# Sample-token projections with the tokens as stationary operand, in four PSUM quadrants, of a two-layer hybrid decoder step

## The chip, the cores and the metric

One Trainium2 chip; the program runs on one of its cores. The metric is the device time of one execution in microseconds, the median of several runs.

## The reference

One inference step of a two-layer decoder on two groups that share the weights: a prompt (2048 tokens) and sample tokens (8 sequences of 4, so 32 tokens). Layer 0 is gated linear attention with 4 heads, layer 1 sliding-window grouped-query attention with 4 groups; between them shared keys and values are projected once.

```python
u = rmsnorm(h, norm_g)                 # (tokens, 1024), prompt and sample alike
proj = u @ w_in                        # layer 0: q 512, k 512, v 2048, gate 2048, g_low 16
log_a = log_sigmoid(g_low @ w_gate2 + b_gate) / 16
o, state = gla_recurrence(q / sqrt(128), k, v, log_a, state0)
h = h + (rmsnorm(o) * silu(gate)) @ w_out          # w_out (2048, 1024)
k, v = rope(rmsnorm(rmsnorm(h) @ w_k)), rmsnorm(h) @ w_v      # 4 KV heads of 64
q, gate = split(rmsnorm(h) @ b_w_in)   # layer 1: 2048 + 2048
h = h + (attend(q, k, v, sinks) * silu(gate)) @ b_w_out
```

The change concerns `u @ w_in`, `u @ w_k`, `u @ w_v`, `u @ b_w_in` and the two products with `w_out` for the 32 sample tokens.

## The kernel before

All float32 products are made of fp16 pairs: a value is a high part plus a low part, and `PASSES` (L283) gives the three products high x high, high x low, low x high. A matmul takes a stationary operand of up to 128 x 128 (loaded by LDWEIGHTS) and streams a moving operand of up to 512 columns past it into one PSUM bank. PSUM banks go by tags: `pj`, `o` and `tr` have two each, `lev` and `kv` one.

**Stage A** (layer 0): the prompt is cut into 4 blocks of 512 tokens, and the outer loop runs over 4 heads x 4 blocks (`blocks`). Per block `qk_steps` projects q and k, `vg_steps` v and gate, `level_steps` and `decay_steps` prepare the recurrence and `chunk_steps` runs it. After the last block of a head the sample tokens of that head are projected (`SampleA.proj_steps`), while the next head's weights arrive: `Unit.load` fetches float32 halves into the ring `wraw` (three buffers), and ScalarE (L197) and VectorE (L198) split them into `W` tiles. A tile scheduler orders each engine's instructions here. `logs` computes the decay, `glow` the low-rank gate, `u_steps` the norm. Then the first output projection runs over 16 chunks (`a_out`), with the sample's part (`out_sample`) at chunk 7 and its end at chunk 10.

**Stage B** (layer 1): 4 groups x 16 chunks, three chunks in flight. The order of TensorE's instructions is pinned to the program's order (`pin`): `ORDER` deals projections ("f") between scores ("A") and values ("B"). After a chunk's round one step of `boundary` runs, among them a whole group's sample projections (`SampleB.proj_steps`), which use the same `W` tiles as the prompt. The second output projection (`Pair.steps`) has the sample's part as `s_out`.

**The sample's projections** are `sproj_steps` (L631). The weights are stationary, 128 input rows by 128 output columns, and the tokens move. Per output tile of 128 columns and k-tile of 128 rows there are two matmuls: the high weights with the tokens' high and low parts side by side (64 columns), and the low weights with the tokens' high part (32 columns). Eight tiles share a bank; the result stands with output columns on the partitions, and `total` (L650) adds the two halves on ScalarE (L656) and VectorE (L657). For the heads and groups the loop runs over 8 k-tiles, for the output projections over 16 or 24; `out_sample` (L1086) then turns its result back to tokens on partitions by four transposes per half.

```python
for k in range(nk):
    wide = lambda: mm(out, w(k, 0), a_[:, kts[k]], start=k == 0, stop=k == nk - 1)
    ...
    mm(out[:, 0, :], w(k, 1), a_[:, kts[k], 0, :], start=False, stop=False)
```

Counted over the program: 10 tiles x 8 k-tiles x 2 per A head, 8 x 8 x 2 per B group (12 x 8 x 2 in the first, which has the shared K/V), and the output projections. Other lines that the steps below touch: L101 is the helper `mm`, L104 the helper `tp` (a transpose by identity), L1039 the one fp32 matmul of the program (`psk`), L1175 a 512-column copy out of PSUM in `q_norm`, L1183 the sum on POOL that makes `kT` there, and `att` the sample attention's scores, which write 32 PSUM partitions per sequence.

Of the kernel before, what the change touches and what calls it, by code (L numbers as in the profile page):

```python
# [19 lines left out]
P = 128  # L20
# [54 lines left out]
def _body(tc, nc, cp, sb, ps, dr, i, o):  # L75
# [24 lines left out]
    def mm(*a, **k):  # L100
        return order(nc.tensor.matmul(*a, **k))  # L101
# [159 lines left out]
    class Cols:  # L261
# [18 lines left out]
        def cols(self, n):  # L280
            return [lambda kt, hl, x=x: self(kt, hl, slice(x * P, (x + 1) * P)) for x in range(n)]

# [347 lines left out]

    def sproj_steps(tiles, nk, act_hi_lo, kts=None, bank=("pj", 2)):  # L631

        box = []
        kts = kts or list(range(nk))

        def one(x, w):
            if x % 8 == 0:
                n = min(8, len(tiles) - x)
                box.append(PT(bank[0], [P, 512], bufs=bank[1])[:, : n * 2 * SMP].rearrange("p (x z t) -> p x z t", z=2, t=SMP))
            out = box[x // 8][:, x % 8]  # L640
            a_ = act_hi_lo()
            for k in range(nk):
                wide = lambda: mm(out, w(k, 0), a_[:, kts[k]], start=k == 0, stop=k == nk - 1)
                if k == 0:
                    wide()
                mm(out[:, 0, :], w(k, 1), a_[:, kts[k], 0, :], start=False, stop=False)
                if k > 0:
                    wide()

        def total(dst, x0, x1, scale):  # L650
            for a in range(x0, x1, 1):
                if a == x0 or a % 8 == 0:
                    b = min(x1, a // 8 * 8 + 8)
                    src = box[a // 8][:, a % 8 : b - a // 8 * 8]
                    d = dst[:, a - x0 : b - x0]
                    act(d, src[:, :, 1], AF.Copy, scale=scale)  # L656
                    dve.scalar_tensor_tensor(d, src[:, :, 0], scale, d, ALU.mult, ALU.add)  # L657

        return [lambda x=x, w=w: one(x, w) for x, w in enumerate(tiles)], total

# [8 lines left out]
    class SampleA:  # L669
# [3 lines left out]
        def proj_steps(self):  # L673
            w = self.w
            st, total = sproj_steps([w.q, w.k] + w.v.cols(4) + w.g.cols(4), KT, lambda: uTs)

            def fin():
                self.qkv = T("sqk", [P, 6, SMP], F32, 1)
                total(self.qkv, 0, 6, DESC * SQ)
                self.sg = T("ssg", [P, 4, SMP], F32, 1)  # L680
                total(self.sg, 6, 10, 1.0)
                silu2(self.sg)

            if self.h == 0:
                st.append(lambda: glow(uTs, SMP, gls))
            return st + [fin]

# [254 lines left out]
    for n, (h, j) in enumerate(blocks):  # L942
# [47 lines left out]
        if n == 0:  # L990
# [22 lines left out]
            dve.tensor_copy(lvs, f_)  # L1013
            id3 = C("id3", [96, SMP], F32)
            later(id3, i["c_id3"])
            bm = C("bm", [96, NS], F32)
# [68 lines left out]

    def out_sample(tiles, half, finish_s, kts=None, sc=OSC):  # L1086
        st, total = sproj_steps(tiles, len(kts or range(16)), lambda: ogTs[0], kts, (("lev", "kv")[half], 1))
# [34 lines left out]
    for c in range(lead, tail):  # L1122
        aout[c + 1][0]()
        weave(aout[c][1][0] + aout[c][1][1], some(each))
        if c == 7:
            late_s = [out_sample(w.cols(4), half, a_finish_s) for half, w in enumerate((wo, wo1))]
# [199 lines left out]
    class SampleB:  # L1326
# [3 lines left out]
        def proj_steps(self):  # L1330
            w = self.w
            first = [x for v in w.kv for x in v.cols(NKV)]
            st, total = sproj_steps(w.q.cols(4) + w.g.cols(4) + first, KT, lambda: uTs)

            def fin():
                if first:
                    t = T("sq1", [P, NKV, SMP], F32, 1)
                    total(t, 8, 12, 1.0)
                    nc.sync.dma_start(skvd, t)
                self.qk = T("sqk", [P, 5, SMP], F32, 1)  # L1340
                nc.sync.dma_start(self.qk[:, 0, :], skvd[:, self.g])
                total(self.qk[:, 1:], 0, 4, 1.0)
                self.sg = T("ssg", [P, 4, SMP], F32, 1)
                total(self.sg, 4, 8, 1.0)
                silu2(self.sg)

            return st + [fin]

# [322 lines left out]

    blks = []
    parts = {}
    boundary = []
# [4 lines left out]
    def s_out(half):  # L1679

        cols = [slice(z * P, (z + 1) * P) for z in range(4)]
        right = [k + 2 for k in UP]
        fs, kts = ((0, 2, 5), UP + UP + right) if half else ((0, 3), UP + right)
        return out_sample([lambda k, hl, z=z: wf[fs[k // 8]](k % 8, hl, z) for z in cols], half, b_finish_s, kts, OSCB)
# [78 lines left out]
def consts():  # L1763
# [22 lines left out]
    for tq in range(2):  # L1786
# [9 lines left out]
        "c_lvs": lvs,  # L1796
        "c_id3": np.tile(np.eye(SMP, dtype=np.float32), (3, 1)),
        "c_bm": np.tile((np.arange(SMP)[:, None] // TS == np.arange(NS)[None, :]).astype(np.float32), (3, 1)),
# [45 lines left out]
```

## Time and profile before

| | |
|---|---|
| three runs | 2857.28, 2862.69, 2869.30 us; median 2862.69 |
| profiled execution | 2863.85 us |
| its span, first to last instruction | 2862.1 us |
| mean granted TensorE clock | 0.983 of full speed |
| TensorE (PE) busy | 96% |
| VectorE (DVE), ScalarE (ACT), GpSimd (POOL) busy | 64%, 50%, 37% |
| DMA | 137 GB/s on the mean |

A row of the timeline gives the start of a group of like instructions and the time to the end of the last; since matmuls are pipelined, what a matmul costs in a row of them is the distance of the starts, not its duration. PE stands for matmuls, PEld for the weight loads beside them.

### The profile page before, as it was taken

The page shows a single profiled execution, that of the slowest core. Times are in us where ns is not written, and L with a number is a line of the kernel's source. Part 1 is how long each engine was busy: PE and PEld are TensorE (multiplying, and loading weights), DVE is VectorE, ACT ScalarE, POOL GpSimd, SP SyncE. Part 2 cuts the span into 40 slices and gives each one's busy share as a digit, 9 for nine tenths or more (in the row PEclk, how much of TensorE's full clock was granted, in tenths as well). Part 3 has the DMA queues.
Part 4 walks back from the last instruction along what each step waited for, and adds up shares of the span by engine and source line. Part 5 has one row for each costly group of instructions (what it writes and reads, how often), then busy time and mean ns, then how long its engine had stood idle before and what let it go on. Part 6 is the DMA issues. An engine that isn't in the chain of part 4 may idle for free.

```text
span 2862.1 us, 51609 instructions
## 1 busy us (share of the span) xinstructions
PE 2735.9 (96%) x19070; PEld 1392.4 (49%) x19070; DVE 1845.7 (64%) x3815; ACT 1440.3 (50%) x3385; POOL 1063.6 (37%) x1471
## 2 busy tenths in 40 slices
PE   6899999999999999999899999999999999988999
PEld 3445444444454444444344555555555555543444
DVE  5767787677768775336413666677777766767653
ACT  6655665466546654333313555566666666641110
POOL 1242233222322321116405676666566556530000
PEclk9899999999999999999999999999999999999999
DMA  8351334124312533799975555866877788798651
GB/s 209 90 124 36 100 101 150 38 82 136 115 38 85 171 84 96 180 240 282 233 193 135 108 130 120 203 117 129 173 116 130 157 155 165 151 236 172 125 112 57
DMA packets 774230, 391.78 MB, mean 137 GB/s; under 512 B 629200, under 2 KB 698776, under 8 KB 773944
## 3 DMA queue, kind: packets, MB, share of 16 engines
q1 hardware_dynamic: 761016, 352.75, 54.6%
q0 software_dynamic: 10880, 35.66, 3.4%
q8 instruction: 149, 2.44, 0.4%
q14 instruction: 105, 0.86, 0.1%
q10 hardware_dynamic: 2080, 0.07, 0.0%
HBM read 138.90 MB, written 107.54 MB: 86 GB/s over the span
## 4 chain that ended last, share of the span: by engine, by line
PE 56%; DVE 12%; DMA 11%; ACT 10%; issue 6%; POOL 4%; SPq 1%; DVEq 0%; ACTq 0%; POOLq 0%
PE pj L101 33%; PE o L101 11%; PE tr L101 8%; PE kv L101 3%; ACT o L1279 2%; DMA pst<-v 2%; DVE v L198 2%; ACT v L197 2%; DMA pre<-pst 1%; PE lev L101 1%; DMA wraw<-in_a_w_in_dram 1%; DVE o L1274 1%; DVE W L198 1%; POOL ogT L195 1%; DVE lev L1274 1%
## 5 line engine op out<-in xcount | busy, mean ns | idle before, releaser
L101 PE MATMUL pj<-W,uT 128*128 128x512 f16 x5088 | 1208.1, 383 | 6.6 <-ACT qT L430 2.9
L101 PEld LDWEIGHTS <-uT 128*128 128x128 f16 x6976 | 654.7, 99 | 714.1 <-issue 40.4
L101 PE MATMUL tr<-W,uT 128*128 128x512 f16 x1536 | 365.8, 379 | 0.0
L186 POOL TENSOR_SCALAR rs_m<-ss 128x1 f32<-128x1 f32 (+3 forms) x190 | 46.1, 243 | 685.7 <-ACT og L611 234.0
L101 PEld LDWEIGHTS <-X 128*128 128x128 f16 x2744 | 185.8, 98 | 149.3 <-issue 14.7
L1279 ACT ACTIVATE o<-o,mx 128x256 f32<-128x256 f32 (+1 forms) x384 | 168.5, 439 | 168.1 <-DVE mx L1274 163.6
L1274 DVE CUSTOM_DVE_ANT_0 o<-o,madd,nsink 128x256 f32<-128x256 f32 (+1 forms) x384 | 184.0, 479 | 48.3 <-PE o L101 44.0
L101 PE MATMUL pj<-uT,W 128*128 128x512 f16 (+1 forms) x912 | 186.0, 354 | 27.0 <-DMA uT<-ogT 24.3
L198 DVE SCALAR_TENSOR_TENSOR v<-o,v 128x512 f16<-128x512 f32 (+1 forms) x192 | 128.8, 671 | 102.0 <-ACT v L197 82.0
L187 POOL TENSOR_TENSOR rs_r<-rs_m,mhalf 128x1 f32<-128x1 f32 (+2 forms) x186 | 184.8, 994 | 14.4
L101 PEld LDWEIGHTS <-W 128*128 128x128 f16 x2448 | 128.0, 98 | 113.1 <-issue 18.5
L101 PEld LDWEIGHTS <-v 128*128 128x128 f16 x976 | 95.2, 98 | 116.0 <-DMA v<-ogd 1.9
L508 POOL TENSOR_TENSOR E<-bt 128x256 f32<-128x256 f32 x96 | 73.9, 770 | 198.4 <-DVE X L195 124.8
L195 POOL TENSOR_TENSOR ogT<-og,ogT 128x512 f16<-128x512 f32 x68 | 88.0, 1295 | 154.4 <-ACT ogT L194 142.5
L101 PEld LDWEIGHTS <-sth 128*128 128x128 f16 x2080 | 111.4, 99 | 52.3 <-DMA sth<-v 12.2
L101 PEld LDWEIGHTS <-sg 128*128 128x128 f16 x800 | 78.6, 99 | 107.5 <-DMA sg<-ogd 12.3
L101 PE MATMUL o<-gl,X 128*128 128x256 f16 (+1 forms) x768 | 114.9, 273 | 5.5 <-DMA X<-qe 5.5
L197 ACT ACTIVATE v<-o 128x512 f16<-128x512 f32 (+1 forms) x192 | 111.3, 579 | 11.1 <-DMA sth<-v 7.6
L101 PE MATMUL kv<-rmask,sth 128*128 128x64 f16 x1984 | 107.0, 194 | 10.1 <-DMA sth<-v 9.2
L101 PE MATMUL kv<-rmask,pst 128*128 128x64 f16 x992 | 102.4, 194 | 9.3 <-DMA pst<-v 9.3
L1279 ACT ACTIVATE lev<-lev,mx 128x256 f32<-128x256 f32 (+1 forms) x128 | 56.5, 441 | 103.3 <-DVE mx L1274 101.2
L101 PE MATMUL pj<-W,v 128*128 128x512 f16 x448 | 104.2, 379 | 1.1 <-DMA v<-ogd 1.1
(468 smaller groups left out, 5092.5 us busy)
## 6 DMA issues: line engine op xcount, KB each, us to landing
pre<-pst POOLq DMA_DIRECT2D x72, 256.0 KB, 3.4
W<-pre SPq DMA_DIRECT2D x36, 512.0 KB
ogd<-ogT SPq DMA_DIRECT2D x68, 256.0 KB
wraw<-in_a_w_in_dram SPq DMA_DIRECT2D x64, 256.0 KB
wraw<-in_b_w_in_dram SPq DMA_DIRECT2D x64, 256.0 KB
oge<-ogT SPq DMA_DIRECT2D x64, 256.0 KB
wraw<-in_a_w_out_dram SPq DMA_DIRECT2D x32, 256.0 KB
X<-in_x_prompt_dram SPq DMA_DIRECT2D x32, 256.0 KB
```

The source lines that it names most:

```text
L101: return order(nc.tensor.matmul(*a, **k))
L186: pool.tensor_scalar(m[:n, :k], ss, a, b, ALU.mult, ALU.add)
L187: pool.tensor_tensor(r[:n, :k], m[:n, :k], mhalf[:n, :k], ALU.pow)
L195: eng.tensor_tensor(lo, src, hi, ALU.subtract)
L197: act(hi, src, AF.Copy, scale=sc)
L198: dve.scalar_tensor_tensor(lo, src, sc, hi, ALU.mult, ALU.subtract)
L508: pool.tensor_tensor(Ev[:, :, 0, :], ref, btv[:, :, 0, :], ALU.subtract)
L1274: dve.tensor_tensor_reduce(pm[:, z], pm[:, z], madd.rearrange("p a b -> p (a b)")[:, (2 - nk) * P :], -0.125, nsink[:, g * GRP + h : g * G ...
L1279: act(pm[:, z], pm[:, z], AF.Exp, scale=-1.0, bias=nm_[:, h : h + 1], accum_out=bx["sum"][:, h : h + 1])
```

## The change

The roles are exchanged. The 32 tokens become the stationary operand (32 columns), the weights move, 512 columns at a time (256 for an A head's q and k, which share a `W` tile). The products of all k-tiles and passes are dealt in turn to the four 32-partition quadrants of one bank (`z = x % 4 * SMP`), so a bank holds four partial sums of [32 tokens, 512 columns], one under the other. `evacuate` copies the bank to an `E` tile (fp32). To sum the four and put the columns back on partitions, `turn` multiplies each 128 columns of it, as stationary fp32 operand, with `id4`, four 32 x 32 identities under each other: one fp32 matmul per 128 columns. For the output projections, where tokens belong on the partitions, one fp32 matmul with `id4` as the stationary and the 512 columns as the moving operand sums the quadrants in place of the four transposes.

The `turn` of a block stands after the next block's matmuls, and a head's or group's last one behind the first steps of the next projection: in stage A after three steps of the next head's q projection, in stage B at the third "f" of the next round (`pend`). The constant `c_id3` of 96 partitions becomes `c_id4` of 128.

```diff
-    def sproj_steps(tiles, nk, act_hi_lo, kts=None, bank=("pj", 2)):
+    def sproj_block(w, ncol, act_hi_lo, kts, bank=("pj", 2)):
+        todo = [(n, k, a, b) for n, k in enumerate(kts) for a, b in PASSES]
         box = []
+        def part(x0):
+            if not box:
+                box.append(PT(bank[0], [P, 512], bufs=bank[1])[:, :ncol])
             a_ = act_hi_lo()
+            for x in range(x0, min(x0 + 24, len(todo))):
+                n, k, a, b = todo[x]
+                z = x % 4 * SMP
+                mm(box[0][z : z + SMP], a_[:, k, a, :], w(n, b), start=x < 4, stop=x + 4 >= len(todo))
+        def evacuate(scale):
+            t = T("E", [P, 512], F32, 2)
+            act(t[:, :ncol], box[0], AF.Copy, scale=scale)
+            return t
+        return [lambda x0=x0: part(x0) for x0 in range(0, len(todo), 24)], evacuate
+    def sproj_steps(blocks, act_hi_lo, done):
+        made, out = [], []
+        def turn(x):
+            n = blocks[x][1] // P
+            pt = PT("tr", [P, 4, SMP], bufs=2)
+            for z in range(n):
+                mm(pt[:, z, :], made[x][:, z * P : (z + 1) * P], id4, start=True, stop=True)
+            done(x, pt[:, :n])
+        def one(x):
+            w, ncol, scale = blocks[x]
+            st, evacuate = sproj_block(w, ncol, act_hi_lo, range(KT))
+            run(st)
+            made.append(evacuate(scale))
+            if x:
+                turn(x - 1)
+        return [lambda x=x: one(x) for x in range(len(blocks))] + [lambda: turn(len(blocks) - 1)]
...
# SampleA
+            def done(x, pt):
+                act((self.qkv[:, :2], self.qkv[:, 2:], self.sg)[x], pt, AF.Copy)
+                if x == 2:
+                    silu2(self.sg)
+            st = sproj_steps([(qk, 2 * P, DESC * SQ), (w.v, 512, DESC * SQ), (w.g, 512, 1.0)], lambda: uTs, done)
...
# the loop over blocks
-            for f in samp.proj_steps():
-                f()
+            sproj = samp.proj_steps()
+            run(sproj[:-1])
         if nxt:
-            for f in nxt.qk_steps():
-                f()
+            qks = nxt.qk_steps()
+            run(qks[:3] + (sproj[-1:] if last else []) + qks[3:])
...
# out_sample
         def fin():
-            t = T(("ssg", "sqk")[half], [P, 4, SMP], F32, 1)
-            total(t, 0, 4, sc)
+            t = evacuate(sc)
             pt = PT("tr", [SMP, 512], bufs=2)
-            for x in range(4):
-                tp(pt[:, x * P : (x + 1) * P], t[:, x, :], idf)
+            mm(pt, id4, t, start=True, stop=True)
             finish_s(half, pt)
...
# SampleB
+            return sproj_steps([(x, 512, 1.0) for x in kv + [w.q, w.g]], lambda: uTs, done)
...
# the loop of stage B
-                boundary += [lambda sm=sm: run(sm.proj_steps())] + sm.steps()
+                pst = sm.proj_steps()
+                boundary += [lambda pst=pst: (run(pst[:-1]), pend.append(pst[-1]))] + sm.steps()
...
                 seen += 1
+                if pend and seen == 3:
+                    pend.pop()()
```

On TensorE, at the end of the second A head (a row reads output<-moving,stationary and the output's partitions x columns), before:

```order
L101 MATMUL o_6405<-v_6085,Sh_6145 128x512
L101 LDWEIGHTS W_2677
L101 MATMUL pj_6148<-uTs,W_2677 128x64
L101 MATMUL pj_6148<-uTs,W_2677 128x32
...
L101 MATMUL pj_6277<-uTs,W_3871 128x64
L101 MATMUL kv_6395<-v_6085,ke_6140 128x512
...
L101 MATMUL tr_7059<-gl_165,w_8_164 128x512
L101 MATMUL pj_6321<-uT_156,W_5708 128x512
```

and in the changed program, where `E_...` with `id_1589` is a `turn`:

```order
L101 MATMUL o_6263<-v_6014,Sh_6074 128x512
L101 LDWEIGHTS uTs
L101 MATMUL pj_6079<-W_2677,uTs 32x256
...
L101 MATMUL kv_6253<-v_6014,ke_6069 128x512
L101 MATMUL pj_6106<-W_3549,uTs 32x512
...
L101 MATMUL pj_6137<-W_3800,uTs 32x512
L101 MATMUL tr_6164<-id_1589,E_6131 128x32 x4
L101 MATMUL pj_6170<-uT_156,W_5637 128x512
...
L101 MATMUL tr_6183<-id_1589,E_6162 128x32 x4
L101 MATMUL tr_6197<-gl_165,w_8_164 128x512
```

Seven of the recurrence's matmuls (`kv`, `o`) now stand between the q/k block and the v block, each block has a bank of its own, and two `turn`s stand on either side of the next head's q projection (17 matmuls of it come first).

On ScalarE at the same place, before (L197 splits a weight half, L656 is the sample's evacuation):

```order
L197 ACTIVATE W_6638<-wraw_6639,gsa 128x512
L197 ACTIVATE W_6638<-wraw_6643,gsa 128x512
L197 ACTIVATE W_6647<-wraw_6648,gsa 128x512
L656 ACTIVATE sqk_6310<-pj_6148 128x192
L197 ACTIVATE W_6647<-wraw_6652,gsa 128x512
L656 ACTIVATE ssg_6313<-pj_6148 128x64
```

and in the changed program (L644 is `evacuate`, L690 the copy in `done`):

```order
L197 ACTIVATE W_6496<-wraw_6497,gsa 128x512
L197 ACTIVATE W_6496<-wraw_6501,gsa 128x512
L644 ACTIVATE E_6104<-pj_6079 128x256
L197 ACTIVATE W_6505<-wraw_6506,gsa 128x512
L608 ACTIVATE og_6285,ss_6286<-o_6263 128x512
L197 ACTIVATE sth_6274<-st_6257 128x512
L197 ACTIVATE W_6505<-wraw_6510,gsa 128x512
L644 ACTIVATE E_6131<-pj_6106 128x512
L690 ACTIVATE sqk_6077<-tr_6133 128x64
```

The fourth weight half's split stood between the two evacuations before; now it stands ahead of the v block's evacuation (`E_6131`).

On TensorE in stage B, at the second group's sample projections in the changed program:

```order
L101 MATMUL pj_20270<-W_18541,uTs 32x512
L101 MATMUL tr_20297<-id_1589,E_20268 128x32 x4
L101 MATMUL o_20309<-gl_15119,X_20005 128x256
...
L101 MATMUL pj_20320<-W_18527,uT_13377 128x512
L101 MATMUL tr_20327<-id_1589,E_20295 128x32 x4
```

The q block's `turn` follows the gate block at once; the gate block's comes after the next round's first scores (four matmuls) and four matmuls of its projection.

## Rows read from the trace of the kernel before

**Rows 1.** The page, busy time, share of the span and instructions of each engine
```profile
PE 2735.9 (96%) x19070; PEld 1392.4 (49%) x19070; DVE 1845.7 (64%) x3815; ACT 1440.3 (50%) x3385; POOL 1063.6 (37%) x1471
```

**Rows 2.** The page, the chain that ended last, shares by engine
```profile
PE 56%; DVE 12%; DMA 11%; ACT 10%; issue 6%; POOL 4%; SPq 1%; DVEq 0%; ACTq 0%; POOLq 0%
```

**Rows 3.** Groups by line and shape, TensorE: busy us, mean ns | idle before
```profile
L101 PE MATMUL pj<-uTs,W 128*128 128x64 f16 x608 | 34.6, 189 | 0.0
...
L101 PE MATMUL pj<-uTs,W 128*128 128x32 f16 x608 | 34.0, 177 | 0.0
```

**Rows 4.** Timeline, stage B: start us, us, engine, what [idle before <-releaser]
```profile
1873.95 3.64 PE L101 MATMUL pj<-uTs,W 128*128 128x64 f16 x128
...
1877.43 0.60 PE L101 MATMUL o<-gl,X 128*128 128x256 f16 x4
1877.50 0.63 ACT L194 ACTIVATE qe<-kT 128x512 f16<-128x512 f32 x1 [1.55 <-POOL kT L1183]
...
1877.87 3.62 PE L101 MATMUL pj<-W,uT 128*128 128x512 f16 x16
...
1881.32 0.22 PE L101 MATMUL kv<-rmask,sth 128*128 128x64 f16 x2
```

**Rows 5.** Timeline, the second A head
```profile
557.59 4.51 PE L101 MATMUL pj<-uTs,W 128*128 128x64 f16 x160
...
561.94 0.59 PE L101 MATMUL kv<-v,ke 128*128 128x512 f16 x2
```

**Rows 6.** Timeline, TensorE at the sample attention; its weight loads by shape
```profile
1773.86 1.24 PE L101 MATMUL pj<-W,uT 128*128 128x512 f16 x5
1775.03 0.30 PE L101 MATMUL lev<-Sh,sq 128*32 128x128 f16 x8
1775.27 0.21 PE L101 MATMUL lev<-sK,sq 128*128 128x32 f16 x2
...
L101 PEld LDWEIGHTS <-sq 128*32 128x32 f16 x64 | 1.3, 94 | 5.8 <-issue 5.7
```

**Rows 7.** Timeline at L1039, and that line's loads
```profile
156.45 0.29 PEld L1039 LDWEIGHTS tr<-skT,sq 8*128 8x128 f32 x2 [0.42 <-issue]
...
156.76 1.50 PE L101 MATMUL tr<-uT,ogTs 128*96 128x512 f16 x6
...
L1039 PEld LDWEIGHTS tr<-skT,sq x2: 181/182/184, 156.4 to 156.6; 8*128 8x128 f32 x2
```

**Rows 8.** Timeline, fp32 transposes on TensorE at two places
```profile
418.15 0.43 PE L104 MATMUL tr<-idf,pst 32*128 32x32 f32 x4
418.51 0.39 PE L101 MATMUL o<-sth,qe 128*128 128x512 f16 x1
...
1604.91 0.60 PE L104 MATMUL tr<-idf,sqk 128*32 128x128 f32 x4
1605.35 0.60 PE L101 MATMUL o<-gl,X 128*128 128x256 f16 x4
```

**Rows 9.** Chain of waits through the second A head: start us, us, what
```profile
558.42 0.02 issue
...
559.98 3.30 DMA wraw<-in_a_w_in_dram
...
563.29 0.73 ACT W L197
...
564.99 5.14 PE pj L101 x23
```

**Rows 10.** Groups by line and shape, ScalarE
```profile
L1175 ACT ACTIVATE E<-pj 128x512 f32<-128x512 f32 x64 | 37.6, 587 | 7.7 <-PE pj L101 4.6 <-PE o L101 3.1
```

**Rows 11.** Waits of TensorE: us in total, times, longest
```profile
PE pj L101 <- DVE ssg L657: 2.3, 3, 1.1
```

**Rows 12.** Timeline, TensorE in the first output projection
```profile
1329.11 0.28 PE L101 MATMUL kv<-ogTs,uT 128*128 128x64 f16 x5
1330.62 0.48 PE L101 MATMUL kv<-ogTs,uT 128*128 128x64 f16 x11 [1.23 <-issue]
```

More of the change, by code (lines that the diff above doesn't have):

```diff
@@ L629, in spill_halves @@
         nc.sync.dma_start(ogd2[c].rearrange("p a k x -> p (a k) x")[:, :, g * 256 : (g + 1) * 256], ot.rearrange("p a (k x) -> p (a k) x", k=2))
-    def sproj_steps(tiles, nk, act_hi_lo, kts=None, bank=("pj", 2)):
+    def sproj_block(w, ncol, act_hi_lo, kts, bank=("pj", 2)):
+        todo = [(n, k, a, b) for n, k in enumerate(kts) for a, b in PASSES]
         box = []
[L634 to L640, printed above, removed]
-            a_ = act_hi_lo()
[L642 to L659, printed above, removed]
@@ L674, in proj_steps @@
             w = self.w
[L675 to L682, printed above, removed]
+            self.qkv = T("sqk", [P, 6, SMP], F32, 1)
+            self.sg = T("ssg", [P, 4, SMP], F32, 1)
+            qk = lambda k, hl: w.qk[k // 4](k % 4, hl, ALL)
+            def done(x, pt):
[3 more added lines that the diff above has]
+            st = sproj_steps([(qk, 2 * P, DESC * SQ), (w.v, 512, DESC * SQ), (w.g, 512, 1.0)], lambda: uTs, done)
             if self.h == 0:
-                st.append(lambda: glow(uTs, SMP, gls))
-            return st + [fin]
+                st.insert(3, lambda: glow(uTs, SMP, gls))
+            return st
         def steps(self):
@@ L958, in _body @@
             samp = SampleA(h, cur.w)
-            for f in samp.proj_steps():
-                f()
+            sproj = samp.proj_steps()
+            run(sproj[:-1])
         if nxt:
-            for f in nxt.qk_steps():
-                f()
+            qks = nxt.qk_steps()
+            run(qks[:3] + (sproj[-1:] if last else []) + qks[3:])
+        elif last:
+            run(sproj[-1:])
         if late:
@@ L1013, in _body @@
             dve.tensor_copy(lvs, f_)
-            id3 = C("id3", [96, SMP], F32)
-            later(id3, i["c_id3"])
+            id4 = C("id4", [P, SMP], F32)
+            later(id4, i["c_id4"])
+            id3 = id4[:96]
             bm = C("bm", [96, NS], F32)
@@ L1084, in a_out, with out_sample @@
         return load, out
-    def out_sample(tiles, half, finish_s, kts=None, sc=OSC):
-        st, total = sproj_steps(tiles, len(kts or range(16)), lambda: ogTs[0], kts, (("lev", "kv")[half], 1))
+    def out_sample(w, half, finish_s, kts=None, sc=OSC):
+        st, evacuate = sproj_block(w, 512, lambda: ogTs[0], kts or range(16), (("lev", "kv")[half], 1))
         def fin():
-            t = T(("ssg", "sqk")[half], [P, 4, SMP], F32, 1)
-            total(t, 0, 4, sc)
+            t = evacuate(sc)
             pt = PT("tr", [SMP, 512], bufs=2)
-            for x in range(4):
-                tp(pt[:, x * P : (x + 1) * P], t[:, x, :], idf)
+            mm(pt, id4, t, start=True, stop=True)
             finish_s(half, pt)
@@ L1125, in _body @@
         if c == 7:
-            late_s = [out_sample(w.cols(4), half, a_finish_s) for half, w in enumerate((wo, wo1))]
+            late_s = [out_sample(w, half, a_finish_s) for half, w in enumerate((wo, wo1))]
             for st in late_s:
@@ L1331, in proj_steps, with done @@
             w = self.w
[L1332 to L1336, printed above, removed]
+            kv = list(w.kv)
+            def done(x, pt):
+                if x < len(kv):
                     t = T("sq1", [P, NKV, SMP], F32, 1)
-                    total(t, 8, 12, 1.0)
+                    act(t, pt, AF.Copy)
                     nc.sync.dma_start(skvd, t)
[L1340 to L1347, printed above, removed]
+                elif x == len(kv):
+                    self.qk = T("sqk", [P, 5, SMP], F32, 1)
+                    nc.sync.dma_start(self.qk[:, 0, :], skvd[:, self.g])
+                    act(self.qk[:, 1:], pt, AF.Copy)
+                else:
+                    self.sg = T("ssg", [P, 4, SMP], F32, 1)
+                    act(self.sg, pt, AF.Copy)
+                    silu2(self.sg)
+            return sproj_steps([(x, 512, 1.0) for x in kv + [w.q, w.g]], lambda: uTs, done)
         def steps(self):
@@ L1679, in s_out @@
     def s_out(half):
-        cols = [slice(z * P, (z + 1) * P) for z in range(4)]
         right = [k + 2 for k in UP]
         fs, kts = ((0, 2, 5), UP + UP + right) if half else ((0, 3), UP + right)
-        return out_sample([lambda k, hl, z=z: wf[fs[k // 8]](k % 8, hl, z) for z in cols], half, b_finish_s, kts, OSCB)
+        return out_sample(lambda k, hl: wf[fs[k // 8]](k % 8, hl), half, b_finish_s, kts, OSCB)
     for t in range(-3, NKV * NCH):
@@ L1796, in consts @@
         "c_lvs": lvs,
-        "c_id3": np.tile(np.eye(SMP, dtype=np.float32), (3, 1)),
+        "c_id4": np.tile(np.eye(SMP, dtype=np.float32), (4, 1)),
         "c_bm": np.tile((np.arange(SMP)[:, None] // TS == np.arange(NS)[None, :]).astype(np.float32), (3, 1)),
```

3 lines of the change are left out of this document (1 added, 2 removed).

## The prediction

> **What bounds the kernel now.** I read the page's busy line first [rows 1]: TensorE is busy for 2735.9 of 2862.1 us, so nearly every microsecond that its stream gains or loses is a microsecond of the end. The chain of waits says the same with one reservation [rows 2]: 56% of it is TensorE, the rest waits on other engines and DMA, so a wait that the change adds or removes counts like work. The sum below is therefore kept on TensorE's queue: what is taken out, what is put in, which waits move. VectorE and ScalarE have spare time on the whole and matter only where TensorE waits for them.
>
> What is taken out are the sample tokens' projections. They are 1792 small matmuls: 1216 in the heads and groups, half of 64 and half of 32 moving columns [rows 3], and 576 in the two output projections (256 and 320, counted from the loops: 4 tiles x 16 k-tiles x 2 x 2 halves; 4 x 16 x 2 and 4 x 24 x 2). The timeline gives their price [rows 4]: 128 of them begin at 1873.95 and the next work at 1877.43, 27.2 ns each whether 64 or 32 columns move; a head's 160 take 4.35 us [rows 5].
>
> **The terms.**
> Removed: 1792 x 27.2 ns = **-48.7 us**.
>
> Added, streaming. Per k-tile and block there are three products now with 512 columns (256 in the q/k block), each in the quadrant after the last one's. Counted over the loops: 624 of 512 columns and 96 of 256. What they cost depends on whether four quadrants stream at once, and the trace has one place that does this, the sample attention's scores [rows 6]: eight matmuls with a stationary of 32 columns and 128 moving columns, two per quadrant. They begin at 1775.03 and the next full-width work at 1775.27, 0.24 us. One after the other, at 0.055 us for 128 columns (half of the 0.11 us that a 256-column matmul takes [rows 4]), they would need 0.44 us. So they overlap, and a round of four costs about what one full matmul costs, 0.216 us for 512 columns (16 in 3.45 us, [rows 4]). 156 rounds x 0.216 + 24 rounds x 0.11 = 33.7 + 2.6 = **+36.3 us**.
>
> Added, entering and leaving the quadrants. In [rows 6] five full matmuls start at 1773.86, which ends at 1774.94; full-width work goes on at 1775.27. Of these 0.33 us two rounds of 0.055 are streaming; 0.22 us is the price of one excursion. From the order of the changed program: three per A head (the q/k, v and gate blocks are parted by other work), one in the first output projection, two for the first B group and one for each other, two in the second output projection, and one for each of the four closing fp32 sums, which also write 32 partitions: 24 x 0.22 = **+5.3 us**.
>
> Added, the fp32 sums. `turn` issues one fp32 matmul per 128 output columns, 40 in the A heads and 36 in the B groups. The only fp32 matmul of the old trace that is not a transpose stands at L1039, and one call is two weight loads and two matmuls [rows 7]. Its two loads, 182 ns each, cover 0.29 us, so the second starts 0.11 us after the first; both pairs with the way out take 0.31 us (156.45 to 156.76). fp32 transposes go at 0.11 us with 128 moving columns (four from 1604.91 to 1605.35); with 32 moving columns four take 0.36 us, 0.0625 each once half an excursion is taken off for the way out of their 32 rows [rows 8]. I take the spacing of the loads, 0.109 per pair, since L1039 is the same operation with as many weight columns: 76 x 2 x 0.109 = **+16.6 us**. Bounds: 0.0625 per pair, the transposes' (-7 us), and 0.155, half of 0.31 (+7 us).
>
> The four closing sums move 512 fp32 columns, four times a 128-column transpose, twice: 4 x 2 x 0.436 = 3.5 us; the 16 transposes that they replace took 16 x 0.109 = 1.7. Net **+1.7 us** (rounded once, 3.49 less 1.74)..
>
> Waits. In an A head the chain runs through a weight load from DRAM [rows 9]: the head's last reads of W at 558.42 free the buffers, ScalarE and VectorE split the first halves, the DMA of the fourth `wraw` takes 3.30 us, ScalarE splits it at 563.29, and only then come the sample's bank evacuations on which the next head's q projection waits until 564.99. In the changed ScalarE order that same fourth split stands ahead of the evacuation of the v block. So I expect the wait to stay in another place: block starts at 557.59, +0.22+0.65 (q/k), +1.51 (seven full matmuls), +0.22+1.30 (v), +0.44 (`turn` of q/k), +0.22+1.30 (gate) puts TensorE at 563.4 before the `turn` of v, while the evacuation can end no sooner than 564.02 + 0.59 [rows 9, 10] = 564.6. That is 1.2 us, against 1.1 that went before. I count old waits (2.3 us in three heads, [rows 11]) against new ones: **0**, with 2 us to either side. In the B groups the evacuation of the second block stands behind a split that waits for POOL's kT until 1877.50 [rows 4], 3.55 us after the block's start; the `turn` that needs it comes after 0.22 + 12 rounds (2.59) + 0.87 + 0.44 + 0.86 = 5.0 us, and 3.55 + 0.63 + 0.59 = 4.8 is sooner: covered, by 0.2 us only. If that cover is gone, four times some tenths are lost. The first output projection has a hole of 1.23 us in its small matmuls for which the trace shows no releaser [rows 12]; with 96 long matmuls in place of 256 short ones I expect it gone: **-1.2 us**, bounds -1.2 and 0.
>
> The evacuations themselves (one 512-column copy per block, 0.59 us [rows 10], and a short one behind each `turn`, for several short ones on ScalarE and VectorE) lie beside TensorE's work and cost nothing but the waits above. The last `turn` of each head or group was moved behind 12 or so of the next projection's matmuls; nothing there waits for it early. No DMA is added or moved but the constant, which grows from 96 to 128 partitions.
>
> Sum: -48.7 + 36.3 + 5.3 + 16.6 + 1.7 + 0 - 1.2 = **+10.0 us**. By stage: A heads +1.74 x 4, first output projection -1.5, B groups +1.73 and 3 x +1.07, second output projection -0.5. Against the profiled execution (2863.85 us, 1.2 above the median of the three runs, which spread from 2857.3 to 2869.3) that is **2874 us**, +0.35%. What a measurement can tell from no change is about 0.5%, 14.3 us; so this is "no change", on the slow side.
>
> **A rule against the change.** The row says that a round of four costs one matmul's time; it has two rounds only, and no row here has more. The Trainium skill, "TensorE: Matmul & The Clock Gate", section "Measured speedup vs the span model", measured less than fourfold: 3.07 times for four packed row tiles of 512 columns, 2.38 for three column tiles; by that the streaming would take 36.3 x 4 / 3.07 = 47.3 us, an estimate, and the total would be near 2885.
>
> **Rivals.**
> *The rounds are longer, slower than before.* If each quadrant's new weights are not loaded behind the stream that uses the old ones, a round is a full matmul plus a load. The 32-column loads of the sample attention last 94 ns [rows 6]; 180 rounds x 0.094 = +16.9 us, total 2891 (+1.0%). It decides early: 2877.0, the median plus 0.5%, is passed when a round costs 17 ns more than I say (180 x 17.5 ns = 3.15 us). For it: in [rows 6] only two matmuls follow each other per quadrant. Against: a load after every stream would put the second round 94 ns later, and the 0.24 us there leave no room for that beside the way out. 13%. The Trainium skill, "TensorEngine Tiling (Array Packing)", section "Restrictions and Gotchas", says that column tiling excludes the fast weight load, which points the same way; no run here shows it yet.
> *fp32 dearer.* Each pair 0.155 instead of 0.109: +7, total 2881 (+0.6%), slower. 17%.
> *fp32 cheaper.* Each pair 0.06: total 2867; with the waits in the A heads gone as well 2864. No change. 18%.
> *Quadrants one after the other,* so that the change doesn't do what it says: 624 x 0.216 + 96 x 0.11 = 145 us in place of 36.3, total 2983. [rows 6] speak against it. 3%.
> *Faster.* The sum has no term that could give 24 us; only the other order of the first half's work, which the scheduler lays out anew at some sixty places, could. 4%.
>
> **How the numbers follow.** The forecast's own case has 45%. A sixth of it lies above 2877 us (7), with four fifths of the dear fp32 (14), the long rounds (13) and the serial case (3): slower by over 0.5% gets 37%; faster 4%, rounded up to 5; no change 58%. The range runs from 2861 (cheap fp32, no new waits, a cheaper way in and out) to 2889 (long rounds nearly whole, or dear fp32 with lost cover); the serial case and a faster one stay out.
>
> **What would show it.** In the changed profile: the 24 matmuls of a 512-column block in 1.30 us (more than 1.40: the rounds are longer); 0.87 us for four `turn` matmuls (0.5 or 1.25: the rivals); about 0.1 us of idle weight loading at each edge of a block; a wait of about a microsecond before the v block's `turn` in each A head, named after ScalarE; no wait of that kind in the B groups. TensorE's sample work should add up to some 62 us where 50.4 stood (48.7 and 1.7). The prediction is wrong if rounds overlap less than fourfold, if the sums cost half or double, or if another wait of over 1 us stands behind an evacuation.

## The result, and the profile after

The changed kernel takes 2871.5 us in the median of 14 runs (2864.53 to 2878.92), the kernel before 2862.8 us in 14 runs beside it: ratio 1.0031, 95% interval 1.0020 to 1.0041, or +8.7 us. The forecast was 2874 us and "no change, on the slow side". A second series (experiment 1) gave 1.0027, 1.0011 to 1.0042.

The page's busy line and chain, which answer to [rows 1] and [rows 2]:

```profile
PE 2739.9 (96%) x18142; PEld 1373.2 (48%) x18142; DVE 1841.6 (64%) x3790; ACT 1451.1 (51%) x3406; POOL 1063.1 (37%) x1471
...
PE 58%; DVE 11%; DMA 10%; ACT 9%; issue 6%; POOL 4%; SPq 1%; ACTq 0%; DVEq 0%; POOLq 0%
```

TensorE issues 928 matmuls fewer and is busy 4 us longer. The profiled execution took 2864.53 us with a span of 2862.8, hardly more than before (2863.85 and 2862.1). It is the fastest of its 14 runs: its mean granted clock was 0.988 where that of before was 0.983, which is some 70 against 100 us at 1.2 GHz, the lower of the two levels. There 512-column matmuls follow each other every 0.427 us in this trace (from 1386.82 on), at 2.4 GHz every 0.216, so the difference can hide up to 15 us (an estimate, half of it). So totals are compared by medians, and the two traces place by place.

The timeline of TensorE through the second A head (start us, us, engine, what, [idle before <-releaser]), which answers to [rows 5]:

```profile
556.85 0.84 PE L101 MATMUL pj<-W,uTs 128*32 128x256 f16 x24
557.62 0.61 PE L101 MATMUL kv<-v,ke 128*128 128x512 f16 x2
...
559.24 1.48 PE L101 MATMUL pj<-W,uTs 128*32 128x512 f16 x24
560.65 0.63 PE L101 MATMUL tr<-id,E 128*128 128x32 f32 x4
561.21 1.48 PE L101 MATMUL pj<-W,uTs 128*32 128x512 f16 x24
562.94 1.08 PE L101 MATMUL tr<-id,E 128*128 128x32 f32 x8 [0.25 <-ACT E L644]
563.85 3.83 PE L101 MATMUL pj<-uT,W 128*128 128x512 f16 x17
...
567.52 0.97 PE L101 MATMUL tr<-id,E 128*128 128x32 f32 x8
568.33 0.38 PE L101 MATMUL tr<-gl,w 96*128 96x512 f16 x1
```

By the distance of the starts the q/k block takes 0.77 us, the v block 1.41, and a `turn` of four fp32 matmuls (the trace shows each as two) 0.81 us (567.52 to 568.33). The wait before the v block's `turn` is there and is named after ScalarE, but it is 0.25 us long, not 1.2. The chain of waits through this head, which answers to [rows 9], has the same steps as before, but the load takes 2.70 us in place of 3.30, and begins 2.1 us after the block's start in place of 2.4:

```profile
558.95 2.70 DMA wraw<-in_a_w_in_dram
```

The second B group in the same view, which answers to [rows 4]; its first `turn` here is that of the q block:

```profile
1876.94 2.77 PE L101 MATMUL pj<-W,uTs 128*32 128x512 f16 x48
1880.15 1.08 PE L101 MATMUL tr<-id,E 128*128 128x32 f32 x8 [0.43 <-ACT E L644]
1881.07 0.60 PE L101 MATMUL o<-gl,X 128*128 128x256 f16 x4
```

And the first output projection, which answers to [rows 12], with the first wait behind it:

```profile
1330.95 2.77 PE L101 MATMUL lev<-W,ogTs 128*32 128x512 f16 x48
1333.55 1.47 PE L101 MATMUL kv<-uT,ogTs 128*32 128x512 f16 x24
1334.84 1.47 PE L101 MATMUL kv<-W,ogTs 128*32 128x512 f16 x24
1336.24 1.04 PE L101 MATMUL pj<-W,sg 128*128 128x512 f16 x4
...
1384.63 1.03 PE L101 MATMUL pj<-W,sg 128*128 128x512 f16 x2 [6.77 <-DMA sg<-ogd]
...
1399.19 5.34 PE L101 MATMUL o<-uT,sg 128*128 128x512 f16 x24
```

48 products take 2.60 us and 24 take 1.29: 54 ns each, four times the rate of a full matmul (0.216 us). The hole of 1.23 us is gone. The wait for `sg` is in the waits of the kernel before too, in the first line here (us in total, times, longest); the second is the changed kernel's:

```profile
PE pj L101 <- DMA sg<-ogd: 10.9, 2, 9.4
```

```profile
PE pj L101 <- DMA sg<-ogd: 7.5, 2, 6.8
...
PE tr L101 <- ACT E L644: 1.7, 5, 0.4
```

By stage, from the starts of the sample blocks in the traces (us; "again" is the second profile of the changed kernel, from experiment 1):

| from, to | before | after | again | forecast of the difference |
|---|---|---|---|---|
| start, first A block | 283.2 | 281.1 | 283.0 | 0 |
| A heads, to the first output projection's block | 1041.5 | 1049.8 | 1049.8 | +7.0 |
| to the first B block | 256.1 | 250.4 | 251.4 | -1.5 |
| B groups, to the second output projection's block | 982.0 | 985.2 | 983.7 | +4.9 |
| to TensorE's end | 295.2 | 292.2 | 294.4 | -0.5 |

### The profile page after: what moved, and what is told of

It is laid out like the page before. It is cut to its first block, busy times and chain, and to the rows that moved or that the text cites. A ratio compares the mean times of both kernels' runs of the same rounds, so it can differ in the third digit from the quotient of the medians.

```text
span 2862.8 us, 49759 instructions
## 1 busy us (share of the span) xinstructions
PE 2739.9 (96%) x18142; PEld 1373.2 (48%) x18142; DVE 1841.6 (64%) x3790; ACT 1451.1 (51%) x3406; POOL 1063.1 (37%) x1471
## 4 chain that ended last, share of the span: by engine, by line
PE 58%; DVE 11%; DMA 10%; ACT 9%; issue 6%; POOL 4%; SPq 1%; ACTq 0%; DVEq 0%; POOLq 0%
PE pj L101 34%; PE o L101 11%; PE tr L101 8%; PE kv L101 3%; ACT o L1291 2%; DVE v L198 2%; DMA pst<-v 2%; ACT v L197 1%; PE lev L101 1%; DVE o L1286 1%; DMA pre<-pst 1%; DMA wraw<-in_a_w_in_dram 1%; POOL ogT L195 1%; DVE lev L1286 1%; DMA X<-qe 1%
## 5 line engine op out<-in xcount | busy, mean ns | idle before, releaser
L101 PEld LDWEIGHTS <-uT 128*128 128x128 f16 x6720 | 645.0, 98 | 705.8 <-issue 33.3
L101 PEld LDWEIGHTS <-W 128*128 128x128 f16 x912 | 84.9, 103 | 106.5 <-issue 17.2
L197 ACT ACTIVATE v<-o 128x512 f16<-128x512 f32 (+1 forms) x192 | 111.1, 579 | 8.1 <-DMA sth<-v 4.7
L101 PE MATMUL kv<-rmask,pst 128*128 128x64 f16 x992 | 101.5, 194 | 11.0 <-DMA pst<-v 10.9
L248 POOL DMA_DIRECT2D pre<-pst x72 | 50.3, 699 | 147.2 <-DVE pst L198 135.9
```

Source lines behind the costliest of these rows:

```text
L197: act(hi, src, AF.Copy, scale=sc)
L248: nc.gpsimd.dma_start(self.pre[:, :, half * 512 : half * 512 + 512], t)
```

## The experiments

Each ratio is against the kernel before, timed beside it; what is said of places is from the run's own profile.

**1. The same kernel again.** No edit.

> The changed kernel itself, for a second profile. Theory (its first profiled execution was its fastest by the luck of TensorE's clock, which was at 1.2 GHz for 49 us after the first sample block, where the kernel before had 73): a span near 2870 with 60 to 75 us at 1.2 GHz; the sample blocks as in the first profile, 1.30 us for 24 products, 0.81 to 0.92 for four turns. Rival (the change raises the clock): again some 50 us, and a span near 2863.

2869.35 us, ratio 1.0027 (1.0011 to 1.0042); span 2866.2 at clock 0.987, or some 75 us at 1.2 GHz in all, 55 of them after the first sample block. That lies between the two theories. Over the eight runs here the mean clock is 0.9860, over the 23 of the kernel before beside them 0.9851, with single runs between 0.983 and 0.987: that the change raises the clock is neither shown nor excluded. What repeats is the A heads' +8.3 us and the blocks.

**2. Six in a row in each quadrant.**

```diff
-                z = x % 4 * SMP
-                mm(..., start=x < 4, stop=x + 4 >= len(todo))
+                per = len(todo) // 4
+                z = x // per * SMP
+                mm(..., start=x % per == 0, stop=x % per == per - 1)
```

> The same products with the same quadrants, but six (12, 18) in a row in one quadrant before the next quadrant's turn. Theory (the gain rests on four different quadrants streaming at once): a 512-column block of 24 takes between 4.5 us (21 of 24 one after the other at 0.216, three joints overlapping) and 5.2 us, where 1.30 stood; over 624 matmuls of 512 columns and 96 of 256 that is +94 to +109 us, total 2966 to 2981. Rival (what counts is only that a stationary of 32 columns is short, the dealing is idle): 1.30 us a block, total 2871.

2896.59 us, 1.0129 (1.0101 to 1.0158): +36 us against before, +27 to +29 against the change, where +94 at least was expected. Both theories fail. The timeline in the first output projection tells why:

```profile
1340.19 7.35 PE L101 MATMUL lev<-W,ogTs 128*32 128x512 f16 x45
1347.16 0.39 PE L101 MATMUL kv<-uT,ogTs 128*32 128x512 f16 x1
1347.37 0.38 PE L101 MATMUL lev<-W,ogTs 128*32 128x512 f16 x1
1347.39 0.38 PE L101 MATMUL kv<-uT,ogTs 128*32 128x512 f16 x1
```

The program has all 48 products of `lev` ahead of the first of `kv`. In the records `kv`'s first product, in quadrant 0, starts while three of `lev`, in quadrant 3, have not started. Matmuls of another quadrant overtake those that wait for their own. A block of 24 takes 2.7 us, in the A heads and also in stage B, where TensorE's order is pinned, so that another order from the tile scheduler is not the reason. That is what 24 x 0.216 = 5.2 us leaves if at each of the three changes of quadrant some four products run ahead of the queue (3 x 4 x 0.216 = 2.6); for 72 products the same count gives 13.0, and 13.1 was measured.

**3. Two quadrants at a time.**

```diff
-                z = x % 4 * SMP
-                mm(..., start=x < 4, stop=x + 4 >= len(todo))
+                per = len(todo) // 2
+                z = (x // per * 2 + x % 2) * SMP
+                mm(..., start=x % per < 2, stop=x % per + 2 >= per)
```

> Two quadrants alternate in the first half of a block, the other two in the second half. Theory (a round costs one full matmul, however many quadrants share it): 12 rounds x 0.216 = 2.6 us for a 512-column block, in all 312 x 0.216 + 48 x 0.11 = 72.7 us of streaming, +36 us, total 2908. Rival (a quadrant's next weight load waits for its stream, hidden until now behind the other three): +0.094 us a round more, 360 x 0.094 = +34 us, total 2942.

2879.14 us, 1.0068 (1.0046 to 1.0090), +11 to +12 against the change. +36 was too much for the same reason: a block of 24 takes 1.85 us, not 2.6, since the second pair of quadrants begins before the first has ended. In the last output projection the changes of pair weigh least:

```profile
2794.47 4.51 PE L101 MATMUL kv<-uT,ogTs 128*32 128x512 f16 x48
2798.81 2.76 PE L101 MATMUL kv<-W,ogTs 128*32 128x512 f16 x24
2801.50 0.61 PE L101 MATMUL pj<-uT,sth 128*128 128x512 f16 x2
```

72 products in 7.03 us: 36 rounds of two at 0.216 would be 7.8. No round shows an added 0.094 for the weight load.

**4. One quadrant.** This separates overtaking from a product that is short by itself.

```diff
+                mm(box[0][:SMP], a_[:, k, a, :], w(n, b), start=x == 0, stop=x == len(todo) - 1)
+                if x == 0:
+                    for z in range(1, 4):
+                        mm(box[0][z * SMP : z * SMP + SMP], zz, w(n, b), start=True, stop=True)
```

`zz` holds zeros.

> All products of a block go to one quadrant; three products of zeros fill the other three once. Theory (within a quadrant the products follow each other every 0.216 us; in the run with six in a row later quadrants' products overtook earlier ones, some four of them at each change of quadrant): 24 x 0.216 = 5.2 us for a 512-column block, 10.4 and 15.6 for 48 and 72, in all 145 us where 36 stood; some 10 us of it vanish in the first output projection's waits, total 2960 to 2980. Rival (matmuls of 32 columns need less than a full one's time even alone in their quadrant): 2.7 us or less a block, total 2900 or less.

2968.77 us, 1.0377 (1.0351 to 1.0403), +100 us against the change, as the theory says of the blocks and the total; that 10 us of it would vanish in the first output projection fails, that stage takes 270 us. The timeline there:

```profile
1368.45 9.88 PE L101 MATMUL lev<-W,ogTs 128*32 128x512 f16 x45
1377.95 0.40 PE L101 MATMUL kv<-uT,zz 128*32 128x512 f16 x3
1378.16 0.59 PE L101 MATMUL lev<-W,ogTs 128*32 128x512 f16 x2
1378.60 5.34 PE L101 MATMUL kv<-uT,ogTs 128*32 128x512 f16 x24
1383.78 5.34 PE L101 MATMUL kv<-W,ogTs 128*32 128x512 f16 x24
```

24 products alone in a quadrant take 5.18 us (1378.60 to 1383.78), in four quadrants 1.29. That is 4.0 times. The Trainium skill, "TensorE: Matmul & The Clock Gate", section "Measured speedup vs the span model", has 2.38 for three column tiles and 3.07 for four row tiles; in a long accumulation these runs show the whole factor. The three zero products overtake two of `lev` here as well.

**5. More excursions.** Two matmuls of zeros, all 128 columns of the array, inside each 24 products.

```diff
+                if x % 24 in (7, 15):
+                    mm(box[0][:, :SMP], idh, zz, start=False, stop=False)
```

> Two full-width matmuls of zeros with 32 columns stand inside each 24 products, 60 in all, added to the same bank. Theory (leaving and entering the quadrants costs 0.09 + 0.10 us whenever it happens): 60 x (0.20 + 0.027) = +13.6 us, total 2885. Rival (the edges seen at the blocks come from the change of bank and of work, not of the width): 60 x 0.027 = +1.6 us, total 2873.

2879.39 us, 1.0069 (1.0049 to 1.0088), +11 us against the change where +13.6 was expected; the interval holds it. The timeline of the second B group:

```profile
1886.38 0.61 PE L101 MATMUL pj<-W,uTs 128*32 128x512 f16 x8
1886.92 0.19 PE L101 MATMUL pj<-zz,idh 128*128 128x32 f16 x1
1887.04 0.61 PE L101 MATMUL pj<-W,uTs 128*32 128x512 f16 x8
1887.59 0.19 PE L101 MATMUL pj<-zz,idh 128*128 128x32 f16 x1
1887.71 1.05 PE L101 MATMUL pj<-W,uTs 128*32 128x512 f16 x16
```

Eight products and a break take 0.67 us (1887.04 to 1887.71), of which 0.43 us are two rounds and 0.03 the zeros: 0.21 us for leaving and coming back, whatever stands between.

**6. Each `turn` matmul twice.**

```diff
                 mm(pt[:, z, :], made[x][:, z * P : (z + 1) * P], id4, start=True, stop=True)
+                mm(pt[:, z, :], made[x][:, z * P : (z + 1) * P], id4, start=True, stop=True)
```

> Each fp32 matmul of the turns is issued twice, 76 more. Theory (they cost 0.20 us each on TensorE's queue, and nothing covers them): +15.4 us, less up to 1 us of the waits before the v blocks' turns in the A heads, which the longer turn of q and k covers: +14.4, total 2886. Rival (they lie in waits that would be there anyway, as before the v blocks' turns): +5 us or less.

2887.01 us, 1.0096 (1.0072 to 1.0120): +18 to +20 us against the change; the forecast of +14.4 lies within the two intervals, the rival's 5 does not. The timeline of the second B group:

```profile
1896.01 1.97 PE L101 MATMUL tr<-id,E 128*128 128x32 f32 x16
1897.81 0.60 PE L101 MATMUL o<-gl,X 128*128 128x256 f16 x4
```

1.80 us where the single `turn` took 0.92 (1880.15 to 1881.07): nothing covers it. The first three A heads took 280 us on the mean where the change's take 276, which is 2 us a head more than the doubled matmuls. In the second of them TensorE waits 11 us in all, 7 in the change, and not for the turns: 2.5 us for `kT` and 2.4 us for `ke` stand out. Why these waits moved stays open.

**7. The `turn` behind its own block.**

```diff
-            if x:
-                turn(x - 1)
+            turn(x)
```

> Each turn stands right behind its own block instead of behind the next block or the next projection's first steps. Theory (the delay hides the evacuation): TensorE waits some 0.9 us (a 0.59 us copy with its way there and back) before 9 turns in the B groups and 8 to 12 in the A heads, +15 to +19 us, total 2888; less where the scheduler finds other work in the A heads, down to +8. Rival (ScalarE's queue is what the turns wait for, and the place of the turn changes nothing): within 3 us of 2871.

2882.26 us, 1.0076 (1.0056 to 1.0097), +13 us against the change, of which the waits show 8. The timeline of the second B group, and the line on the evacuation in the waits of TensorE:

```profile
1886.48 1.48 PE L101 MATMUL pj<-W,uTs 128*32 128x512 f16 x24
1888.94 1.08 PE L101 MATMUL tr<-id,E 128*128 128x32 f32 x8 [0.98 <-ACT E L644]
```

```profile
PE tr L101 <- ACT E L644: 9.8, 13, 1.8
```

9.8 us in place of 1.7, of which 7.2 stand before the nine turns of the B groups. There the later place of the `turn` is what hides the evacuation; the first three A heads (276.3 us each, 276.2 in the two profiles of the change) do not need it. The rest of the +13 us lies with the first output projection (257.9 us, 250.4 and 251.4 in the change), which this edit does not touch.

**8. Only the output projections in the new scheme.** Heads and groups as before the change.

> The new scheme in the two output projections alone; heads and groups are as before the change. Theory (by stage): first output projection -1.5, second -0.5 against the kernel before: total 2861, ratio 0.9993. Rival (the slower 9 us come from the output projections or from a new order of the first half): total 2866 or more.

2862.09 us, 1.0002 (0.9987 to 1.0016): no change, as the theory says. The first three A heads are back at 273.6 us each. But the stage of the first output projection takes 256.8 us, no less than before, though its hole is gone. First the start of its block and the work behind its wait for `sg` in the kernel before, then the timeline of this one:

```profile
1324.75 3.65 PE L101 MATMUL lev<-ogTs,W 128*128 128x64 f16 x128
...
1399.08 5.34 PE L101 MATMUL o<-uT,sg 128*128 128x512 f16 x24
```

```profile
1326.95 2.77 PE L101 MATMUL lev<-W,ogTs 128*32 128x512 f16 x48
...
1385.04 1.03 PE L101 MATMUL pj<-W,sg 128*128 128x512 f16 x2 [10.04 <-DMA sg<-ogd]
...
1398.98 5.34 PE L101 MATMUL o<-uT,sg 128*128 128x512 f16 x24
...
1412.23 1.04 PE L101 MATMUL tr<-E,id 128*32 128x512 f32 x2 [2.73 <-ACT E L647]
```

Up to the work behind the wait for `sg` this kernel needs 72.0 us (1326.95 to 1398.98), before it was 74.3: 2.3 us are saved and kept. Then TensorE waits for the evacuations before the two closing sums, 2.73 and 0.31 us, and they are lost again. In the two profiles of the change the first part takes 68.2 and 67.6 us, with shorter waits for `sg` (7.5 and 8.7 us; 11.2 here, 10.9 before), and the waits before the closing sums are 0.35 and 1.91 us. In experiment 2, with 9.6 us more of products ahead, 1.4 us of the wait for `sg` were left, TensorE never fell to 1.2 GHz in this stage (13.7 us here), and the stage took 252.5 us.

**9. fp16 pairs for the fp32 sums.**

```diff
-            t = T("E", [P, 512], F32, 2)
-            act(t[:, :ncol], box[0], AF.Copy, scale=scale)
+            t = T("E", [P, 2, 512], F16, 2)
+            split((t[:, 0, :ncol], t[:, 1, :ncol]), box[0], scale)
...
-                mm(pt[:, z, :], made[x][:, z * P : (z + 1) * P], id4, start=True, stop=True)
+                for b in range(2):
+                    mm(pt[:, z, :], made[x][:, b, z * P : (z + 1) * P], id4h, start=b == 0, stop=b == 1)
```

Scales are moved so that the pairs fit fp16; the closing sums are changed alike.

> The evacuated block is split into an fp16 high and low part (ScalarE, then VectorE), and each fp32 matmul of the turns and closing sums becomes two fp16 ones. Theory (the fp32 sums are the largest avoidable term): the 76 turns go from 0.20 us to 2 x 0.027, -11 us; four closing sums from 0.98 to 0.45 us, -2 us; the evacuation ends 0.6 us later, and where its cover was short (four A heads, the B groups' q turn) that comes back: +3 to +5. Total 2862 (2858 to 2866), level with the kernel before. Rival (what the turns cost is their weight load of 128 columns, which an fp16 pair needs as well): 0.1 us for each of the two, total 2871.

2874.43 us, 1.0040 (1.0026 to 1.0055). No gain. The matmuls cost what the theory says (27 ns each, 4.1 us for all turns), so 13 us of TensorE's work are gone from the turns alone; TensorE's waits took them:

```profile
PE tr L101 <- DVE E L198: 8.4, 10, 1.7
PE tr L101 <- ACT E L197: 8.0, 8, 2.1
```

16.4 us where 1.7 stood. By stage, the A heads take 1056.1 us (1049.8 in the change) and the first output projection 257.1, while from the first B block to the end it is 1269.6 (1277.4): the gain in stage B is lost ahead of it. In the second A head the clock follows; TensorE's busy time by windows (columns: window, us, PE busy, clock, DMA share, GB/s):

```profile
562.00:564.40 2.40, 1.16 (x12) 1.00 0.41 118
564.40:567.80 3.40, 3.40 (x10) 0.50 0.35 123
```

TensorE idled for half of 2.4 us and then ran 3.4 us at 1.2 GHz.

**10. In addition q's sum with tokens on the partitions.** One such sum replaces a `turn` and four transposes in each B group.

```diff
+            if x == row:
+                pt = PT("tr", [SMP, 512], bufs=2)
+                for b in range(2):
+                    mm(pt, id4h, made[x][:, b], start=b == 0, stop=b == 1)
```

> As with the fp16 pairs, and in the four B groups the q block is summed like the output projections, tokens on the partitions (two fp16 matmuls of 512 columns, 0.43 us), which also makes four fp32 transposes (0.44 us) needless that turned it back. Theory: 4 x (0.22 + 0.44 - 0.43) = -1 us against the fp16 pairs, and one transpose bank and a copy less on ScalarE: total 2861. Rival (waits, not TensorE's columns, set what is left): no difference from the fp16 pairs.

2874.55 us, 1.0049 (1.0035 to 1.0062): no gain to be seen, but the 1 us of the theory is too little to be told from none in these runs, so neither is shown.

**11. Pairs in stage B and the output projections, A heads as before the change.** The edits of 9 without SampleA's, whose old code is put back.

> The A heads as before the change, the B groups and the output projections with the changed scheme and fp16 pairs in place of the fp32 sums. Theory (A heads cost 2 us more each under the change, and the pairs' later evacuation made that 4; in stage B the pairs took 8 us from the changed kernel): heads as before, -8 us against before from the first B group on: total 2854, ratio 0.997. Rival (what stage B gained was the clock's luck in one profile; by the blocks only -5 of the fp32 turns and -1 of the closing sums are sure, and +5 of the change stands against them): 2861, ratio 0.9995.

2854.49 us, 0.9974 (0.9961 to 0.9986): faster than both kernels, as the theory says. From the first B block to the end it takes 1271.2 us, before 1277.2, the change 1277.4 and 1278.1. What it still waits in the second B group, by the timeline:

```profile
1873.43 0.34 PE L101 MATMUL tr<-id4h,E 128*128 128x32 f16 x7 [0.36 <-DVE E L198]
...
1876.30 0.34 PE L101 MATMUL tr<-id4h,E 128*128 128x32 f16 x7 [1.21 <-DVE E L198]
```

A rival is the clock. Against the change the gain is not the clock's: from the first B block on, both profiles have 24 us at 1.2 GHz, and this kernel is 6.2 us shorter. The profile of before has 41 us there, so of the 6.0 us against it the clock can have all. Over the runs the mean clock is 0.9876 here and 0.9851 in the 23 of the kernel before beside them, some 14 us less at 1.2 GHz, worth up to 7 us by half (an estimate). That this kernel is faster than the one before is measured; how much of it the cheaper sums give directly and how much the clock stays open.

**12. Later turns in the B groups.** As 11, with q's turn taken out of the gate block's step.

```diff
-            if x:
+            if 0 < x < len(blocks) - 1:
                 turn(x - 1)
...
-                boundary += [lambda pst=pst: (run(pst[:-1]), pend.append(pst[-1]))] + sm.steps()
+                boundary += [lambda pst=pst: (run(pst[:-2]), pend.extend(pst[-2:]))] + sm.steps()
...
-                if pend and seen == 3:
-                    pend.pop()()
+                if pend and seen in (2, 6):
+                    pend.pop(0)()
```

> As the best run so far, but in the B groups both turns stand later: q's at the second and the gate's at the sixth piece of the next round's projection. Theory (the fp16 pairs wait for the low half on VectorE: 0.36 to 0.38 us before q's turn and 1.21 to 1.23 before the gate's, 5.4 us in the four groups): these waits go, total 2849, ratio 0.9955. Rival (the copies stay longer in E and the round's other copies wait for its two buffers): no gain, 2854 or more.

2852.46 us, 0.9968 (0.9952 to 0.9984). The waits before q's turn went, those before the gate's fell, in the second group to this row of the timeline:

```profile
1875.67 0.34 PE L101 MATMUL tr<-id4h,E 128*128 128x32 f16 x7 [0.76 <-DVE E L198]
```

By the rows 3 of the 5.4 us are saved; the times of 11 and 12 cannot be told apart. Here the mean clock is 0.9866 against 0.9857 beside it, some 5 us less at 1.2 GHz, so that at most 3 of the 9 us are the clock's.

## Why the prediction was right, and where it was not

**The terms on TensorE held.** Over all products the starts, from the first of a block to the work behind it, give 39.2 us, and some 0.1 us go to each of 20 entries: 41.2, where 40.7 was said (36.3, and 20 excursions at 0.22). One excursion is 0.21 us [experiment 5]. The turns come to 17.1 us (16.6 said), a `turn` of four to 0.81 us, or 0.92 where it comes straight out of the quadrants (0.87 said). The closing sums take 0.98 us each and 0.09 for the entry, 4.3 in all (4.4). Sum 62.6 us against 50.4, as forecast ("some 62").

**Quadrants overlap, and by the whole factor**: 54 ns for each product, no load between the rounds. The rivals "longer rounds" and "one after the other" are out, and experiment 4 gives the price of the latter (+100 us against the change, +109 said). My reason was thinner than the result: two rounds in [rows 6].

**fp32 at 0.1 us per pair** was the right choice between the bounds; experiment 6 shows it as a cost on the path. "fp32 cheaper" and "fp32 dearer" are out with it. Experiment 9 does not say what cheap sums alone would give, since its evacuations end later as well.

**The waits were mis-sized one by one.** The step "1.2 us before the `turn` of v" in each A head measured 0.25 in the second, and 0.37 at most in any: the chain that I had read in [rows 9] is there, but the load in it was 0.6 us shorter. All five waits for an evacuation come to 1.7 us, in the second profile four come to 2.4; both lie within the 2 us that the term was given, and that they do is in part luck, since two kinds of them I had put at nothing. One is the 0.43 us before the q block's `turn` of the second B group; the cover "by 0.2 us only" was reckoned for the gate block's `turn`, and it held. The other stands before the closing sums of the first output projection: 0.35 us in the first profile, 1.49 and 0.42 in the second, 2.73 and 0.31 in experiment 8.

```profile
1412.40 1.05 PE L101 MATMUL tr<-E,id 128*32 128x512 f32 x2 [1.49 <-ACT E L644]
```

So in one of the two profiles "another wait of over 1 us stands behind an evacuation", which I had named as a sign that the prediction is wrong; it costs 1.5 us, and the sum stands with it.

**By stage the sum was right for partly wrong reasons.** The A heads cost 8.3 us (7.0 said), and so much in both profiles. Of the first output projection I said -1.5 through the hole. The hole went, and experiment 8 is 2.3 us ahead behind the wait for `sg`, but the waits before its closing sums take this back. I had read the hole of [rows 12], not the waits of 10.9 us for `sg` after it nor the evacuation that each closing sum must wait for. In the two profiles of the change this stage is 5 us shorter than before, with shorter waits for `sg` and less time at 1.2 GHz (10.2 and 6.8 us, 13.7 before). Over all runs here it lies between 250 and 260 us (270 with one quadrant); what sets the landing of `sg` stays open. The B groups cost +1.7 to +3.2 (4.9 said), the last stage -0.8 to -3.0, within what the granted clock of single executions does (17 and 23 us at 1.2 GHz in the B groups of the change, 31 before).

## What to carry to other kernels

Count both sides of an exchange of operands in start-to-start slots: here four quadrants made the products cheaper (41 against 49 us), and the sums over the quadrants, which they made necessary, cost 21 us where transposes had cost 1.7. A cheaper instruction may give nothing when its operand takes longer to make; read the waits before and after, and keep the new form only in the stages where other work covers them. Follow a saving to the end of its stage: here 2.3 us were lost again at a wait for an evacuation 13 us further on.

## What the runs showed of the hardware

- Matmuls in different 32-column quadrants overtake each other: in the records a product starts ahead of three earlier ones that wait for their own quadrant, and the time of a block fits some four at each change of quadrant [experiments 2 and 4]. So the dealing need not be perfect: six in a row cost 2.7 us a block, not 5.2.
- Leaving and entering the quadrants costs 0.21 us also for a single matmul of 32 moving columns between [experiment 5].
- An fp32 matmul of 128 stationary and 32 moving columns shows as two pairs of a load and a matmul of 0.10 us each; an fp16 one of the same shape takes 0.027 [the profile after, experiment 9].
